# The out projection's last steps woven with norm, transposes and router in a written order, and low parts moved from GpSimd to VectorE

## The chip, the cores and the metric

The kernel runs on one core of a Trainium2 chip, as one program. The metric is the device time of one execution in microseconds. Besides the timed executions there is one profiled execution, and all rows below are from it. TensorE multiplies matrices, VectorE, ScalarE and GpSimd (POOL in the rows) work elementwise, and SyncE (SP) issues the loads of weights.

## What is computed

The reference is a chain of two blocks on 256 tokens of width 1024, all in float32. The first block has two layers of this form (the second block, attention with pooling and dense feed-forward parts, is untouched by the main part of the change):

```
mix = jnp.concatenate([ret_o, swa_o, mla_o], axis=-1) @ w_out[l]
x = layer_norm(DEEPNORM_ALPHA * x + mix, ln1_g[l], ln1_b[l])
ffn = grouped_moe(x, router_w, router_bias, exp_w_gate_up[l], exp_w_down[l])
x = layer_norm(DEEPNORM_ALPHA * x + ffn, ln2_g[l], ln2_b[l])
```

The three parts of `mix` are a retention, a sliding-window attention and a latent attention. The mixture of experts has 16 experts in 4 groups:

```
scores = jax.nn.sigmoid((t @ router_w).astype(jnp.float32))
biased = scores + router_bias.astype(jnp.float32)
grp = biased.reshape(T, N_GROUPS, EXPERTS_PER_GROUP)
grp_score = jnp.sum(lax.top_k(grp, TOP_K)[0], -1)
sel_group = jnp.argmax(grp_score, -1)
...
h = jnp.einsum('td,edf->tef', t, w_gate_up)
a = jax.nn.silu(h[..., :D_EXPERT]) * h[..., D_EXPERT:] * gates[..., None].astype(h.dtype)
y = jnp.einsum('tef,efd->td', a, w_down)
```

Each token picks one group, and two experts within it.

## The kernel before

Tokens are held in two halves t = 0, 1 of 128 each. All products are made to float32's accuracy from two parts of each operand, a high part (rounded) and a low part (the rest), in three passes: high by high, low by high, high by low. A weight tile is loaded (`raw`, 1 MB, line 336), its high part `whi` is made on ScalarE (L350) and its low part `wlo` on VectorE (L351), in pieces of 128x1024, of which five are held at a time. Two pieces come from one `raw`.

The stage in question lies between attention and experts, once in each layer. The out projection (`gemm_wide("wo", ...)`, results `oo`, one bank for each token half and half of the columns) runs over 8 contraction steps. Its last TAIL = 3 steps are grouped: all three for t = 0, then all three for t = 1, so that half 0 ends early. Then come, for each half, the residual on VectorE (L899), the statistics of the norm (`ln_stats`, L570 to L573, and a reciprocal square root of ten small ops, `ln1...`, L480 to L489), and 8 transposes of the token tile on TensorE (`trx`, L1053), copied to `rT` on ScalarE. `centre` normalizes the tokens on ScalarE (L1039), makes their high part there (L1040, `xs`) and the low part on GpSimd (L1041, `xs`).

`route` makes the logits from the transposes (`lg`, 16 matmuls in two passes each, 32 rows in the trace), keeps TensorE's clock up with 24 idle matmuls (`keep_clock(WARM[0])`, `idle`), takes the tanh on ScalarE, finds the groups on VectorE by small ops (L948 to L967; `rGb` is the choice of group), counts tokens of each group on TensorE (`cn`), and gives each token a slot. WARM[1] = 12 more idle matmuls follow. `pm` (L1064) is the permutation made of the slots. Then the tokens are gathered by group on TensorE (`og`, 8 tiles of four matmuls: low and high part, both halves), and `affine_evac` brings each tile to high part `xgh` (ScalarE, L605), a plain copy `aff` (VectorE, L606) and low part `xgl` (VectorE, L607). Products of expert 0 (`ogu<-whi,xgh` and so on, 24 matmuls for each expert's gate and up part) begin between the og.

After that the program has a branch (`tc.If(most > P)`) for the case that a group holds more than 128 tokens. The number is read by the engines from `mi`, which VectorE computes. Behind it stand the products that spread gates over slots (`gp`), the transposes `trp`, expert 1's products, the down products of expert 0 (`yg`), then expert 2 and so on.

The order of instructions on each engine is set by a scheduler that goes by priorities, except inside `tc.manual_schedule`, where the engines named take them in the order in which the code is written. `tc.issue_after` puts what it encloses behind a given instruction.

Of the kernel before, what the change touches and what calls it, by code (L numbers as in the profile page):

```python
# [19 lines left out]
P = 128  # L20
T = 256
D = 1024
KT = 8
# [343 lines left out]
def build(ctx: ExitStack, tc: tile.TileContext, ap, tap=None, parts=("b1", "b2")):  # L367
# [57 lines left out]
    def gemm_wide(name, x, nk, outs, order=None, nseg=1, tail=1):  # L425


        groups = [[i] for i in range(nk - tail)] + [list(range(nk - tail, nk))]
        for group in groups:
            ws = [[W.next(name) for s in range(nseg)] for i in group]  # L430
            for t in range(2):
                for i, w in zip(group, ws):
                    kt = order[i] if order else i
                    xa = tuple(h[:, kt, t * P : (t + 1) * P] for h in x[:2])
                    for s in range(nseg):
                        for o, c0, c1 in outs[t][s::nseg]:
                            mm3(o, xa, (w[s][0][:, c0:c1], w[s][1][:, c0:c1]), i == 0, i == nk - 1)
# [164 lines left out]
    def affine_evac(hi, lo, src, g, b, work):  # L602
# [53 lines left out]
    def attention1(l, x, hl, work, cb):  # L656
# [174 lines left out]
        for t in range(2):  # L831
# [4 lines left out]
            G.tensor_tensor(out=gg[:, t, :], in0=th, in1=rep("gn", l), op=ALU.mult)  # L836
# [42 lines left out]
        def score(h, sc):  # L879
# [11 lines left out]
        gemm_wide(  # L891
            "wo", mix, 8, [[(oo[t][n], n * 512, (n + 1) * 512) for n in range(2)] for t in range(2)], OUT_ORDER,
            tail=TAIL,
# [8 lines left out]
        return residual, router  # L902
# [19 lines left out]
    def route(rT, stats, router, work):  # L922


        gw, bs = router
        lg = bank("mm", "lg")
        lgs = work.tile([P, 2, NE], F32, name="lgs")
        for t in range(2):
            o = lg[:, t * NE : (t + 1) * NE]
            for kt in range(KT):  # L930
                last = mm(o, rT[:, t, kt, :], gw[:, kt, :], kt == 0, kt == KT - 1)
        with tc.issue_after(last.ins):
            keep_clock(WARM[0])
        for t in (1, 0):
            V.scalar_tensor_tensor(
                out=lgs[:, t], in0=lg[:, t * NE : (t + 1) * NE], scalar=stats[t][1], in1=bs, op0=ALU.mult, op1=ALU.add
# [8 lines left out]
        S.activation(out=sc.rearrange("p t g e -> p (t g e)"), in_=lgs.rearrange("p t e -> p (t e)"), func=AF.Tanh, scale=0.5)  # L945
        rb = rb5.rearrange("p (g e) -> p g e", g=4)
        for t in range(2):
            V.scalar_tensor_tensor(out=bi[:, t], in0=sc[:, t], scalar=0.5, in1=rb, op0=ALU.mult, op1=ALU.add)  # L948
# [18 lines left out]
        TT(out=G1, in0=key, in1=mx.unsqueeze(2).to_broadcast([P, 2, 4]), op=ALU.is_equal)  # L967
# [8 lines left out]
        last = mm(cn[:, 8:12], one, Gb[:, 1, :], False, True)  # L976
        with tc.issue_after(last.ins):
            keep_clock(WARM[1])
# [38 lines left out]
    def moe(l, residual, router):  # L1017

        with ExitStack() as es:
# [11 lines left out]

            def centre(t):

                mu, rs = stats[t]
                nb = tiny.tile([P, 1], F32, name="nb_ln1", tag="bnnb")
                V.scalar_tensor_tensor(out=nb, in0=mu, scalar=-1.0, in1=rs, op0=ALU.mult, op1=ALU.mult)
                for n in range(2):
                    c = slice(n * 512, (n + 1) * 512)
                    S.activation(out=r[:, t, c], in_=r[:, t, c], func=AF.Identity, scale=rs, bias=nb)  # L1039
                    S.copy(xs[t][:, 0, c], r[:, t, c])  # L1040
                    split = G.tensor_tensor(  # L1041
# [4 lines left out]
            for t in range(2):  # L1046
                r = residual(t)
                stats.append(ln_stats(r, t, "ln1"))
# [554 lines left out]
```

## Time and profile before

| what | value |
|---|---|
| three timed runs | 1735.08, 1733.93, 1735.04 us; median 1735.04 |
| profiled execution | 1737.42 us, its span 1735.6 us |
| TensorE busy | 1673.4 us, 96% of the span |
| VectorE, ScalarE, GpSimd busy | 1278.7, 988.0, 56.2 us |
| TensorE's wait `cn<-rGb` | 3.7 us in each of two layers |

A kernel whose TensorE is busy nearly all the time is read by the few stretches in which it is not, and by the clock it was granted in them: the windows view shows both.

### The profile page before, as it was taken

Reading aid. Unit: us, or ns where it says so; the run is one execution under the profiler, and the core shown is the slowest. Engines: PE = TensorE matmul, PEld = TensorE weight load, DVE = VectorE, ACT = ScalarE, POOL = GpSimd, SP = SyncE. Lnnn points to the kernel's source line nnn. Section 1 sums busy time; section 2 is a strip of 40 time slices with the busy share of each in tenths; the row PEclk is TensorE's granted clock in tenths of the full one; section 3 lists DMA queues with packets and bytes.
Section 4 is the critical chain, followed back from the end, with each engine's and each line's share of the span. In section 5 each row is a group of like instructions: output and inputs, shape, how many; then the busy total and the mean of one; then the engine's idle time right before and its main releaser. Section 6 shows DMA issues by size and latency. Waiting matters only on the chain.

```text
span 1735.6 us, 26627 instructions
## 1 busy us (share of the span) xinstructions
PE 1673.4 (96%) x10190; PEld 1458.9 (84%) x10190; DVE 1278.7 (74%) x2318; ACT 988.0 (57%) x1647; POOL 56.2 (3%) x52
## 2 busy tenths in 40 slices
PE   8998999899999989999999999999999999999997
PEld 8877777797777778999989989998999998988886
DVE  5768999876789987666865676667666775676666
ACT  5645777574577764455565544555555565465553
POOL 0001000200100000000000000000000000100000
PEclk9998999999899999999999999999999999999999
DMA  9432999553279864555533455554455452545540
GB/s 380 148 108 96 344 333 352 188 179 122 74 275 342 329 249 150 191 191 174 184 121 130 170 179 185 194 179 162 174 191 190 148 186 89 193 170 194 191 149 25
DMA packets 49141, 330.93 MB, mean 191 GB/s; under 512 B 5616, under 2 KB 5872, under 8 KB 13424
## 3 DMA queue, kind: packets, MB, share of 16 engines
q1 hardware_dynamic: 47664, 324.68, 51.6%
q10 hardware_dynamic: 1344, 4.49, 0.9%
q8 instruction: 82, 1.34, 0.3%
q14 instruction: 51, 0.42, 0.1%
HBM read 325.74 MB, written 1.05 MB: 188 GB/s over the span
## 4 chain that ended last, share of the span: by engine, by line
PE 67%; DVE 3%; ACT 1%; issue 1%; ACTq 0%; DVEq 0%
PE v L411 14%; PE f L411 14%; PE u L411 14%; PE ogt L411 6%; PE ogu L411 4%; PE oz L411 3%; PE obr L411 3%; PE yg L411 2%; PE ovp L411 2%; PE oq L411 2%; DVE wlo L351 1%; ACT whi L350 1%; PE sc L411 1%; PE po L411 1%; PE opl L411 1%
## 5 line engine op out<-in xcount | busy, mean ns | idle before, releaser
L351 DVE TENSOR_TENSOR wlo<-raw,whi 128x1024 fp32r<-128x1024 f32 (+2 forms) x611 | 736.4, 1212 | 319.0 <-ACT whi L350 303.5
L350 ACT CAST whi<-raw 128x1024 fp32r<-128x1024 f32 (+2 forms) x611 | 629.8, 1034 | 541.1 <-PE v L411 122.6
L411 PE MATMUL f<-fhh,whi 128*128 128x256 f32 x1056 | 196.5, 286 | 1.6 <-DVE fhh L1332 1.6
L411 PE MATMUL v<-xT_hf,whi 128*128 128x512 f32 x528 | 190.7, 399 | 5.4 <-DVE fhp L1329 5.4
L411 PE MATMUL u<-xT_hf,whi 128*128 128x512 f32 x528 | 189.3, 397 | 0.7 <-ACT htok L1314 0.7
L411 PEld LDWEIGHTS f<-fhh,whi 128*128 128x128 f32 x1056 | 166.4, 193 | 6.2 <-DVE fhh L1332 2.3
L411 PE MATMUL f<-fhh,wlo 128*128 128x256 f32 x528 | 149.9, 286 | 0.0
L411 PE MATMUL v<-xT_hf,wlo 128*128 128x256 f32 x528 | 148.5, 281 | 0.0
L411 PE MATMUL u<-xT_hf,wlo 128*128 128x256 f32 x528 | 148.3, 281 | 0.0
L411 PEld LDWEIGHTS v<-xT_hf,whi 128*128 128x128 f32 x528 | 99.7, 189 | 29.7 <-ACT fsl L1325 6.2
L411 PEld LDWEIGHTS u<-xT_hf,whi 128*128 128x128 f32 x528 | 99.1, 188 | 22.8 <-ACT htok L1314 0.9
L411 PE MATMUL ogu<-wlo,xgh 128*128 128x512 f32 x256 | 101.7, 397 | 4.3 <-DVE wlo L351 4.3
L411 PE MATMUL ogu<-whi,xgh 128*128 128x512 f32 x256 | 102.2, 399 | 0.1
L411 PEld LDWEIGHTS f<-fhh,wlo 128*128 128x128 f32 x528 | 101.3, 192 | 0.0
L411 PEld LDWEIGHTS u<-xT_hf,wlo 128*128 128x128 f32 x528 | 99.8, 189 | 1.0
L411 PEld LDWEIGHTS v<-xT_hf,wlo 128*128 128x128 f32 x528 | 100.3, 190 | 0.3
L411 PE MATMUL ogu<-whi,xgl 128*128 128x512 f32 x256 | 100.4, 392 | 0.0
L411 PE MATMUL ogt<-xT_hmx,whi 128*128 128x256 f32 x512 | 97.5, 287 | 0.0
L411 PE MATMUL yg<-whi,hh 128*128 128x512 f32 x256 | 84.6, 391 | 3.4 <-ACT hh L495 3.3
L411 PEld LDWEIGHTS ogt<-xT_hmx,whi 128*128 128x128 f32 x512 | 80.4, 191 | 3.0 <-issue 1.5
L411 PE MATMUL ogt<-xT_hmx,wlo 128*128 128x256 f32 x256 | 73.2, 287 | 0.0
L411 PE MATMUL v<-xT_h,whi 128*128 128x512 f32 x176 | 64.3, 403 | 2.7 <-DVE fhp L1329 2.7
(505 smaller groups left out, 3287.8 us busy)
## 6 DMA issues: line engine op xcount, KB each, us to landing
raw<-in_wflat_dram SPq DMA_DIRECT2D x276, 1024.0 KB, 4.8
raw<-in_wflat_dram SPq DMA_DIRECT2D x10, 960.0 KB, 4.7
raw<-in_wflat_dram SPq DMA_DIRECT2D x4, 992.0 KB, 4.8
gb<-in_rows_dram SPq DMA_DIRECT2D x6, 512.0 KB, 4.7
raw<-in_wflat_dram SPq DMA_DIRECT2D x4, 512.0 KB, 3.2
raw<-in_wflat_dram SPq DMA_DIRECT2D x2, 1008.0 KB, 6.1
raw<-in_wflat_dram SPq DMA_DIRECT2D x2, 976.0 KB, 6.8
raw<-in_wflat_dram SPq DMA_DIRECT2D x4, 384.0 KB, 6.1
```

What stands on the lines that cost most here:

```text
L350: nc.scalar.copy(hi[:, :n], r[:, c : c + n])
L351: self.split = nc.vector.tensor_tensor(out=lo[:, :n], in0=r[:, c : c + n], in1=hi[:, :n].bitcast(F32), op=ALU.subtract)
L411: return TE.matmul(out, lhsT=lhsT, rhs=rhs, start=start, stop=stop, skip_group_check=shared)
```

## The change

The code of the routing stage is written in a fixed order for TensorE and VectorE. `gemm_wide` hands out the last three out-projection steps as functions, so that the residual, transposes and logits of half 0 can stand between the steps of half 1. The reciprocal square root is made once for both halves, on 128x2. Both `centre` come behind the tanh. The low parts of the tokens move from GpSimd to VectorE, behind `pm` (`rest`). In `affine_evac` of this stage every second tile's `aff` moves from VectorE to ScalarE. Outside the stage, three multiplies and sums move from GpSimd to VectorE: the cosine multiply of rope, the retention's `gg`, and the mixer's `msum`.

```diff
+        def step(t, i, w):
+            kt = order[i] if order else i
+            xa = tuple(h[:, kt, t * P : (t + 1) * P] for h in x[:2])
...
+            if defer and group is groups[-1]:
+                return [[lambda t=t, i=i, w=w: step(t, i, w) for i, w in zip(group, ws)] for t in range(2)]
...
         S.activation(out=hi, in_=src, func=AF.Identity, scale=g, bias=b)
-        V.tensor_scalar(out=tmp, in0=src, scalar1=g, scalar2=b, op0=ALU.mult, op1=ALU.add)
+        if turn:
+            S.activation(out=tmp, in_=src, func=AF.Identity, scale=g, bias=b)
+        else:
+            V.tensor_scalar(out=tmp, in0=src, scalar1=g, scalar2=b, op0=ALU.mult, op1=ALU.add)
...
-        G.tensor_tensor(out=dst, in0=src, in1=cosT.unsqueeze(1).to_broadcast(shape), op=ALU.mult)
+        V.tensor_tensor(out=dst, in0=src, in1=cosT.unsqueeze(1).to_broadcast(shape), op=ALU.mult)
...
-            G.tensor_tensor(out=gg[:, t, :], in0=th, in1=rep("gn", l), op=ALU.mult)
+            V.tensor_tensor(out=gg[:, t, :], in0=th, in1=rep("gn", l), op=ALU.mult)
...
-                    split = G.tensor_tensor(
+            def rest(t):
+
+                for n in range(2):
+                    c = slice(n * 512, (n + 1) * 512)
+                    split = V.tensor_tensor(
                         out=xs[t][:, 1, c], in0=r[:, t, c], in1=xs[t][:, 0, c].bitcast(F32), op=ALU.subtract
                     )
...
+            with tc.manual_schedule(engines={mybir.EngineType.PE, V.engine}):
+                for f in steps[0]:
+                    f()
+                r = residual(0)
+                moments(0)
+                steps[1][0]()
+                turned(0)
+                steps[1][1]()
+                logits(rT, 0, lg, router[0])
+                steps[1][2]()
+                r = residual(1)
+                turned(1)
+                moments(1)
+                V.tensor_scalar(out=ve, in0=mv[:, :, 1], scalar1=LN_EPS, scalar2=None, op0=ALU.add)
+                rsqrt_n(ve, rs, 2, 1.0)
+                logits(rT, 1, lg, router[0])
+                keep_clock(WARM[0])
...
+                with tc.high_priority(offset=200):
+                    G1, slot, tot, late = route(lg, rs, router, work)
+                with tc.issue_after(routed.ins):
+                    centre(0)
+                    centre(1)
...
+                rest(0)
+                split = rest(1)
...
-            G.tensor_tensor(out=ms, in0=mg[:, :T], in1=mg[:, T:], op=ALU.add)
+            V.tensor_tensor(out=ms, in0=mg[:, :T], in1=mg[:, T:], op=ALU.add)
```

What this moves on the engines is seen best in their queues. First VectorE between the last attention output (`mixT`) and the second half's statistics, before:

```order
L351 TENSOR_TENSOR wlo<-raw,whi 128x1024
L496 TENSOR_TENSOR mixT<-po,mixT 128x256
L899 SCALAR_TENSOR_TENSOR x_133<-x_133,oo_1318 128x512
L899 SCALAR_TENSOR_TENSOR x_133<-x_133,oo_1319 128x512
L570 BN_STATS st_ln_1470<-x_133 128x6 x2
L571 BN_AGGR mv_ln_1471<-st_ln_1470 128x2
L573 TENSOR_SCALAR ve_ln_1475<-mv_ln_1471 128x1
L480 TENSOR_SCALAR ln10i<-ve_ln_1475 128x1
L351 TENSOR_TENSOR wlo<-raw,whi 128x1024
L481 TENSOR_SCALAR ln10y<-ln10i 128x1
L899 SCALAR_TENSOR_TENSOR x_133<-x_133,oo_1320 128x512
```

and the same place of the changed kernel:

```order
L503 TENSOR_TENSOR mixT<-po,mixT 128x256
L909 SCALAR_TENSOR_TENSOR x_133<-x_133,oo_1318 128x512
L909 SCALAR_TENSOR_TENSOR x_133<-x_133,oo_1319 128x512
L1047 BN_STATS st_ln_1460<-x_133 128x6 x2
L1048 BN_AGGR mv_1432<-st_ln_1460 128x2
L909 SCALAR_TENSOR_TENSOR x_133<-x_133,oo_1320 128x512
L909 SCALAR_TENSOR_TENSOR x_133<-x_133,oo_1321 128x512
L1047 BN_STATS st_ln_1516<-x_133 128x6 x2
```

The two `wlo` shown, and three more around them, are gone from here. VectorE behind the slots, in the changed kernel (L1063 makes the low parts `xs`, L616 is `aff`, L617 `xgl`):

```order
L1107 TENSOR_SCALAR pm<-cperm,rslot 128x512 x2
L1063 TENSOR_TENSOR xs_1430<-x_133,xs_1430 128x512 x2
L1004 TENSOR_TENSOR rpk<-rsc,rG 128x16
L1063 TENSOR_TENSOR xs_1431<-x_133,xs_1431 128x512 x2
L351 TENSOR_TENSOR wlo<-raw,whi 128x1024
L616 TENSOR_SCALAR aff<-og,cols 128x512
L351 TENSOR_TENSOR wlo<-raw,whi 128x1024
L617 TENSOR_TENSOR xgl<-aff,xgh 128x512 x2
L616 TENSOR_SCALAR aff<-og,cols 128x512
L351 TENSOR_TENSOR wlo<-raw,whi 128x1024
L617 TENSOR_TENSOR xgl<-aff,xgh 128x512 x2
```

The pattern goes on to a fourth `wlo` and the eighth `xgl`; behind that stand gate ops with six more `wlo` among them, the third of which is expert 1's first, and then the branch. Before, `pm` was followed by the gate ops, then `aff` and `xgl` with no `wlo` between them, and one `wlo` ahead of the branch. TensorE where the out projection ends, in the changed kernel:

```order
L1073 MATMUL trx<-cperm,x_133 128x128 x8
L411 MATMUL oo_1320<-whi,mixT 128x512
L411 MATMUL oo_1320<-wlo,mixT 128x512
L411 MATMUL oo_1320<-whi,mixT 128x512
L411 MATMUL oo_1321<-whi,mixT 128x512
L411 MATMUL oo_1321<-wlo,mixT 128x512
L411 MATMUL oo_1321<-whi,mixT 128x512
L411 MATMUL lg<-gw,rT 128x16 x8
```

Before, all 16 `trx` and then all 16 `lg` stood behind the last `oo`. Ahead of the branch, TensorE now has 17 of the 24 matmuls of expert 1: one between those of expert 0, and 16 in a row behind them, of which the last four are here:

```order
L411 MATMUL ogu<-wlo,xgh 128x512
L411 MATMUL ogu<-whi,xgl 128x512
L411 MATMUL ogu<-whi,xgh 128x512
L411 MATMUL ogu<-wlo,xgh 128x512
L1161 TENSOR_LOAD mi
L1163 COMPARE_AND_BRANCH
```

Before, none of them stood there: behind expert 0's products came the zeroing of `ya` and then the branch.

## Rows read from the trace of the kernel before

**Rows 1.** The page: busy time, share of the span and instructions of each engine.

```profile
PE 1673.4 (96%) x10190; PEld 1458.9 (84%) x10190; DVE 1278.7 (74%) x2318; ACT 988.0 (57%) x1647; POOL 56.2 (3%) x52
```

**Rows 2.** Timeline of TensorE, layer 0: start, length, operation, idle before and releaser.

```profile
134.37 0.39 PE L411 MATMUL oo<-wlo,mixT 128*128 128x512 f32 x1
134.60 0.39 PE L411 MATMUL oo<-whi,mixT 128*128 128x512 f32 x1
...
136.61 4.04 PE L411 MATMUL lg<-gw,rT 128*128 128x16 f32 x32
140.49 4.15 PE L411 MATMUL idle<-zeros 128*128 128x256 bf16 x24
...
148.53 0.27 PE L411 MATMUL cn<-rGb,cntw 128*128 128x4 bf16 x5 [3.67 <-DVE rGb L966]
148.67 2.72 PE L411 MATMUL idle<-zeros 128*128 128x256 bf16 x12
151.04 4.20 PE L411 MATMUL og<-pm,xs 128*128 128x512 f32 x12
...
166.76 1.92 PE L411 MATMUL gp<-rvs,pm 128*128 128x4 f32 x16 [0.64 <-PEq L1118]
...
174.18 0.50 PE L411 MATMUL yg<-whi,hh 128*128 128x512 f32 x1 [0.71 <-ACT hh L495]
...
179.53 0.39 PE L411 MATMUL ogu<-whi,xgh 128*128 128x512 f32 x1
```

**Rows 3.** Windows: busy time of each engine, granted clock, DMA share, GB/s.

```profile
148.50:151.00 2.50, 2.47 (x17) 1.78 (x17) 2.47 (x22) 0.00 (x0) 0.00 (x0) 0.50 0.00 0
151.00:155.20 4.20, 4.20 (x15) 3.40 (x14) 2.46 (x16) 1.56 (x2) 0.00 (x0) 0.69 0.02 6
...
179.50:200.00 20.50, 20.50 (x93) 16.39 (x92) 19.25 (x20) 16.25 (x20) 0.00 (x0) 1.00 1.00 368
...
465.00:467.50 2.50, 2.48 (x17) 1.79 (x17) 2.47 (x22) 0.00 (x0) 0.00 (x0) 0.50 0.00 0
```

**Rows 4.** Timeline of TensorE, layer 1: cn, and the first matmul of expert 2.

```profile
465.02 0.28 PE L411 MATMUL cn<-rGb,cntw 128*128 128x4 bf16 x5 [3.66 <-DVE rGb L966]
...
497.13 0.39 PE L411 MATMUL ogu<-whi,xgh 128*128 128x512 f32 x1
```

**Rows 5.** Timeline of VectorE, layer 0, from the residual to the permutation.

```profile
135.32 0.68 DVE L899 SCALAR_TENSOR_TENSOR x<-x,oo 128x512 f32<-128x512 f32 x1
...
142.87 0.84 DVE L948 SCALAR_TENSOR_TENSOR rbi<-rsc,rb 128x16 f32<-128x16 f32 x2 [0.52 <-ACT rsc L945]
143.74 1.14 DVE L952 TENSOR_TENSOR rpr<-rbi 128x16 f32<-128x16 f32 x1
...
148.31 0.17 DVE L966 TENSOR_TENSOR rGb<-cperm,rmx 128x8 bf16<-128x8 f32 x1
...
149.29 0.88 DVE L1064 TENSOR_SCALAR pm<-cperm,rslot 128x512 fp32r<-128x512 f32 x2
```

**Rows 6.** Timeline of GpSimd, layer 0: low parts of the tokens.

```profile
142.32 5.02 POOL L1041 TENSOR_TENSOR xs<-x,xs 128x512 fp32r<-128x512 f32 x4 [1.12 <-ACT xs L1040]
```

**Rows 7.** Timeline of VectorE in another stage: one op of the two-column root.

```profile
659.10 0.16 DVE L467 TENSOR_TENSOR rva<-rvb 128x2 f32<-128x2 f32 x1
```

**Rows 8.** Timeline of ScalarE, layer 0: four copies of the transposes.

```profile
135.98 2.04 ACT L1055 COPY rT<-trx 128x512 f32<-128x512 f32 x4
```

**Rows 9.** Timeline of VectorE, layer 0, gathered tokens and weights' low parts.

```profile
155.40 1.52 DVE L606 TENSOR_SCALAR aff<-og,cols 128x512 f32<-128x512 f32 x2
156.84 1.28 DVE L607 TENSOR_TENSOR xgl<-aff,xgh 128x512 fp32r<-128x512 f32 x2
...
168.81 2.35 DVE L351 TENSOR_TENSOR wlo<-raw,whi 128x1024 fp32r<-128x1024 f32 x2
```

**Rows 10.** Groups of GpSimd's instructions: busy us, mean ns of one, idle before.

```profile
L1472 POOL TENSOR_TENSOR msum<-mg 128x256 f32<-128x256 f32 x16 | 12.8, 800 | 207.1 <-DVE mg L1470 207.1
```

**Rows 11.** Waits of TensorE, layer 1's attention stage: us in total, times, longest.

```profile
PE oret L411 <- DVE sT L847: 1.1, 2, 0.6
```

More of the change, by code (lines that the diff above doesn't have):

```diff
@@ L900, in residual @@
             return x
-        return residual, router
+        return residual, router, steps
     def router_weights(l, work):
@@ L920, in router_weights, with logits, route @@
         return gw, sums[:, 1]
-    def route(rT, stats, router, work):
-        gw, bs = router
-        lg = bank("mm", "lg")
-        lgs = work.tile([P, 2, NE], F32, name="lgs")
[L928 to L933, printed above, removed]
+    def logits(rT, t, lg, gw):
+        for kt in range(KT):
+            mm(lg[:, t * NE : (t + 1) * NE], rT[:, t, kt, :], gw[:, kt, :], kt == 0, kt == KT - 1)
+    routed = None
+    def route(lg, rs, router, work):
+        bs = router[1]
+        lgs = work.tile([P, 2, NE], F32, name="lgs")
         for t in (1, 0):
             V.scalar_tensor_tensor(
-                out=lgs[:, t], in0=lg[:, t * NE : (t + 1) * NE], scalar=stats[t][1], in1=bs, op0=ALU.mult, op1=ALU.add
+                out=lgs[:, t], in0=lg[:, t * NE : (t + 1) * NE], scalar=rs[:, t : t + 1], in1=bs, op0=ALU.mult, op1=ALU.add
             )
@@ L975, in route @@
         mm(cn[:, 8:12], one, Gb[:, 0, :], False, False)
-        last = mm(cn[:, 8:12], one, Gb[:, 1, :], False, True)
-        with tc.issue_after(last.ins):
-            keep_clock(WARM[1])
+        mm(cn[:, 8:12], one, Gb[:, 1, :], False, True)
+        keep_clock(WARM[1])
+        TT(out=G1, in0=key, in1=mx.unsqueeze(2).to_broadcast([P, 2, 4]), op=ALU.is_equal)
         tot = w([4], "rtot")
@@ L1015, in route, with moe @@
         return G1, slot, tot, gates
-    def moe(l, residual, router):
+    def moe(l, residual, router, steps):
         with ExitStack() as es:
@@ L1044, in centre, with turned @@
                 return split
-            for t in range(2):
-                r = residual(t)
-                stats.append(ln_stats(r, t, "ln1"))
+            def turned(t):
                 for k4 in range(2):
-                    tr = bank("acc", "trx")
+                    tr = bank("tr", "trx")
                     for j in range(4):
@@ L1053, in moe @@
                         TE.transpose(tr[:, j * P : (j + 1) * P], r[:, t, kt * P : (kt + 1) * P], ident)
-                    with tc.high_priority(offset=200):
-                        S.copy(rT[:, t, 4 * k4 : 4 * k4 + 4, :].rearrange("p k s -> p (k s)"), tr)
-                if t == 0:
-                    centre(0)
-            G1, slot, tot, late = route(rT, stats, router, work)
-            split = centre(1)
-            tap(f"G{l}", G1)
-            pm = work.tile([P, 2, 4, P], F32R, name="pm")
@@ L1063, in moe @@
-            for t in range(2):
-                routed = V.tensor_scalar(
-                    out=pm[:, t].rearrange("p g s -> p (g s)"), in0=iota, scalar1=slot[:, t : t + 1],
-                    scalar2=None, op0=ALU.is_equal,
-                )
+                    S.copy(rT[:, t, 4 * k4 : 4 * k4 + 4, :].rearrange("p k s -> p (k s)"), tr)
+            lg = bank("mm", "lg")
+            rs = work.tile([P, 2], F32, name="rs1")
+            nb = work.tile([P, 2], F32, name="nb1")
+            ve = work.tile([P, 2], F32, name="ve1")
@@ L1078, in moe @@
                     affine_evac(
-                        xgh[:, kt, :], xgl[:, kt, :], o, col("ln1_g", l, kt), col("ln1_b", l, kt), work
+                        xgh[:, kt, :], xgl[:, kt, :], o, col("ln1_g", l, kt), col("ln1_b", l, kt), work, kt % 2
                     )
@@ L1513, in build @@
             cb = work.tile([P, ap["cb1"].shape[1]], F32, name="cb1")
-            residual, router = attention1(l, x, hl, work, cb)
-        r2 = moe(l, residual, router)
+            residual, router, steps = attention1(l, x, hl, work, cb)
+        r2 = moe(l, residual, router, steps)
         xh = ln_hat(r2, "ln2")
```

47 lines of the change are left out of this document (30 added, 17 removed).

## The prediction

> **What bounds the kernel now.** I read the page first: TensorE is busy 96% of the span [rows 1], so a change can pay only in the few places where TensorE stands still or runs slowly. The list of its waits then names the routing stage, once in each of the two layers, and the timeline of TensorE through that stage, layer 0 first, is what the rest is read from. The reader is to see there the end of the out projection (oo), 16 transposes, the router logits (lg), 24 idle matmuls, then 3.67 us in which the counting matmul cn waits for rGb from VectorE, 12 idle matmuls, the gather og, the first products after the branch (gp), and at 179.53 the first matmul of expert 2 [rows 2]. I call that last moment M. Behind it TensorE is busy 20.50 of 20.50 us [rows 3], so a shift of M shifts the end one to one. In layer 1 the cn wait is as long, 316.49 us later, and M is 497.13 [rows 4], or 180.64 by layer 0's time.
>
> The clock is the second thing to see. After the 3.67 us wait the granted share is 0.50 (the 1.2 GHz level) from 148.5 to 151 and 0.69 from 151 to 155.2, and layer 1 shows 0.50 again [rows 3]; twelve idle matmuls take 2.72 us where 24 took 4.15, and the first 12 og take 4.20 us, where passes at the full clock are 0.23 us apart (134.37 to 134.60), or 2.8 us [rows 2]. So the half clock costs 0.65 + 1.4 = 2.1 us a layer.
>
> The third is VectorE before rGb: two small ops take 0.84 and the next 1.14 us, and two more of that size as long, [rows 5] exactly while GpSimd makes the low parts xs, from 142.32 to 147.34 [rows 6]; outside that stretch an op of that size takes 0.17 us (rGb itself). Some 3 us of the cn wait come from that.
>
> **The change, part by part.** *Up to the slots.* TensorE now does 8 transposes and 8 logits steps of token half 0 between the out projection's last steps of half 1. That is half of what lies between the last oo's end, 134.99, and the first idle matmul, 140.49 [rows 2], or 2.8 us, and the oo of half 1 ends so much later: 137.8. VectorE then has the residual (two ops of 0.68 [rows 5], the first partly before that), two statistics of like length, and aggregate: to 140.2. One rsqrt for both halves, ten dependent ops on 128x2, at about 0.2 us each (0.16 busy [rows 7] and a step between): to 142.2. The logits and tanh take to rbi 0.8 to 1.0 us, to 143.1; then the chain to rGb without GpSimd beside it, about ten ops at 0.2: 145.1, against 148.31. TensorE meanwhile: transposes of half 1 to 139.3, two copies rT on ScalarE of 0.51 each [rows 8], eight logits steps of 2.0 us, to 141.9, and 24 idle matmuls, 4.15: 146.05. So cn no longer waits for VectorE; it is the idle matmuls that end last. From cn to the first pm 0.76 us as before, and both pm 0.88 [rows 5]: they end at 147.7 instead of 150.2. **Gain so far 2.5 us, and the half clock of before is gone as well.**
>
> *Behind the slots.* The gain is spent here. VectorE now makes the low parts xs: four ops like xgl, 1.28 for two [rows 9], 2.6 us in all, to 150.3. The five wlo that stood among and ahead of the residual and norm ops (where VectorE's queue had room, since it waited there for oo) now stand behind xs. In the queue from there to the low part of expert 1's first weight piece I count 7 wlo at 1.18 (2.35 for two), 4 aff at 0.76, 8 xgl at 0.64 [rows 9], and some 15 small gate ops at 0.11 (between rGb and the first pm nine steps take 0.98 us [rows 5]): 8.2 + 3.0 + 5.1 + 1.6 = 17.9, to 168.2. Four aff at 0.76 went to ScalarE, otherwise it would be 171.2; ScalarE, busy 57% of the span [rows 1], has time for them. TensorE can run only as far as the eighth xgl, which lies 3 wlo and 13 small ops before that, at 163.2, and two passes on. It then waits with `ogu<-wlo` of expert 1 from about 163.6 to 168.2, **4.6 us (3.5 to 5.2) of new wait in place of the 3.67 us removed**. Queued behind that matmul are 15 more of expert 1, and then the branch, which reads mi; mi itself stands behind two further wlo on VectorE, so it is ready at about 171.0.
>
> From there to M at full clock: 16 passes paced by the two further wlo, to 171.8; 0.64 for the branch, as ahead of gp before; gp at 172.4. From gp to M it was 12.8 us (166.76 to 179.53), of which 17 of expert 1's 24 passes at 0.23 now stand ahead of the branch, 3.9, and the wait for hh, 0.71 [rows 2], is covered by the passes that stand around it: 8.2. **M = 180.6.** If the VectorE ops start as closely as in their densest rows (wlo at 1.14, small ops at 0.09) and pm ends with them, 179.0; if every third of them waits a little for its operand, 181.7. Against 179.53 and 180.64 that is +1.1 and −0.05: together +1.0, bounds −2.2 to +3.2.
>
> *The clock after the new wait.* No row of before has this wait, but the nearest, 3.67 us, was followed by the half clock in both layers. So I take it that TensorE again comes out of 4.6 us at 1.2 GHz. What that cost before was 2.1 us; here the first 16 passes are partly paced by wlo anyway, so I take 1.7 a layer, bounds 0 and 2.5: **+3.4**. The Trainium skill says in "TensorE: Matmul & The Clock Gate", section "What's actually happening", that the throttled clock is the default and that activity releases it; that speaks against this change, since it puts TensorE's idle time in front of dense work and not in front of idle matmuls. The trace agrees, with 0.50 behind the 3.67 us. By the rule the sum is the one below; if the clock stayed up, it would be 3.4 less.
>
> *The rest.* gg moves from GpSimd to VectorE, and its two ops stand between th and the decay product sT, for which TensorE already waits 1.1 us in two times in layer 1 [rows 11]: about 0.3 us more a layer, 0 to 0.6: +0.6. Rope's cosine multiply (four ops) and the mixer's 16 msum (0.80 each on GpSimd [rows 10]) become VectorE work, by xgl's 0.64 for 512 columns an estimated 0.3 for an msum and 1.3 to 1.6 for a rope op. What hides them is that TensorE never waits for either's result; with that cover gone they would cost at most 16 × 0.3 + 4 × 1.5 = 10.8 us. I take 0. The merged rbi, the later G1 and nb are in the chain above.
>
> Sum: +1.0 + 3.4 + 0.6 = +5.0. The profiled execution took 1737.42 us (span 1735.6, and 1.8 around it that the change leaves alone), so it becomes 1742.4; the three timed runs have their median 2.4 below it, 1735.04, so the forecast is **1740.0**.
>
> **The rivals.** *A: the clock stays at 2.4 GHz after the new wait.* Then +1.6, 1736.6, no measurable change (0.2%, 3.5 us, is about what a measurement of this kernel can tell). For it: TensorE has been working, if with gaps, for 10 us before. Against it: both waits of 3.7 us were followed by 0.50. The rule named above would not let this happen.
>
> *B: faster.* The gain of 2.5 us in pm is kept, because the weights' low parts don't end last. The place is the wait for expert 1's wlo; it decides as soon as that wait is under about 2 us, since then there is no half clock either, M falls by 2.5 us in the mean of the layers, and the time is 1735.0 − 5 + 0.6 = 1730.6. If VectorE cost nothing there, TensorE's own work (some 26.3 us from og to M: 28.5 before, from 151.04 to 179.53, less 1.4 of half clock and some 0.8 of waits) would give M = 174.2, 6 us a layer, and about 1724. For it: GpSimd no longer slows VectorE, and four aff at 0.76 left its queue. Against it: 18 us of queued VectorE work, each term from a row, stand between 150.3 and that piece, in an order that can't change at run time.
>
> *C: the moves off GpSimd end last.* sT late by the whole of gg and msum late in part, +2 to +5 on top: 1742 to 1745. Against: TensorE's waits there are short or none.
>
> *D: nothing at all,* both ends cancelling at M: this lies within A's range.
>
> **How the numbers follow.** Forecast 0.47, A and D 0.30, B 0.17, C 0.06. The forecast's own range is 1737 to 1743: a few of its cases lie within 0.2% (0.04), C is slower. So slower 0.49, same 0.33, faster 0.18 (with a little of A's lower end). The range reaches from B's middle to above the forecast's upper bound: 1731 to 1743.5.
>
> **What would show it.** Right: no cn wait for rGb (idle matmuls run into cn); the small ops after tanh at 0.2 us; no GpSimd row there; pm ending near 147.7; then in TensorE's waits `ogu <- wlo`, about 4 to 5 us, once a layer just before the branch, and the granted share 0.5 to 0.7 in the 4 us behind it; M near 182.3 and, in layer 1, 182.3 + 316.5. Wrong: that wait under 2 us, or the share at 1.00 behind it, or pm no earlier than 149 (then copies or tanh are later than summed). If M is as said and the end is not, it is the retention stage or the mixer, and the waits for sT or msum must show it.

## The result and the profile after

The changed kernel takes 1747.8 us (median of 4 runs, 1746.3 to 1750.97), the kernel before beside it 1734.68 (4 runs, 1733.93 to 1735.08). The ratio is 1.0074 (95% interval 1.0058 to 1.0090): slower, and by more than the 1740.0 of the forecast and its range. In a second measurement (e10) the ratio was 1.0086 (1.0069 to 1.0103). The profiled execution of the changed kernel took 1746.3 us with a span of 1744.5, against 1737.42 and 1735.6 before. So the spans differ by 8.9 us and the medians by 13.1. The 4.2 between them come from the profiled runs' places: before's lies 2.7 above the median of its runs here, after's 1.5 below. No trace accounts for that part.

The page first, the same row as [rows 1]: busy time, share of the span and instructions of each engine. GpSimd has shrunk from 56.2 to 18.0 us, and TensorE's busy time has grown by 3.4 us with the same 10190 instructions, which says that some of them ran at a lower clock.

```profile
PE 1676.8 (96%) x10190; PEld 1459.1 (84%) x10190; DVE 1275.8 (73%) x2324; ACT 989.5 (57%) x1653; POOL 18.0 (1%) x20
```

TensorE's timeline through the routing stage of layer 0, to be laid beside [rows 2]:

```profile
137.62 0.40 PE L411 MATMUL oo<-whi,mixT 128*128 128x512 f32 x1
138.11 1.35 PE L1073 MATMUL trx<-cperm,x 128*128 128x128 f32 x8
...
141.52 4.37 PE L411 MATMUL idle<-zeros 128*128 128x256 bf16 x24
...
145.75 0.26 PE L411 MATMUL cn<-rGb,cntw 128*128 128x4 bf16 x5
145.94 1.47 PE L411 MATMUL idle<-zeros 128*128 128x256 bf16 x12
147.17 3.83 PE L411 MATMUL og<-pm,xs 128*128 128x512 f32 x15
...
166.81 0.79 PE L411 MATMUL ogu<-wlo,xgh 128*128 128x512 f32 x1 [3.88 <-DVE wlo L351]
...
173.48 2.00 PE L411 MATMUL gp<-rvs,pm 128*128 128x4 f32 x16 [0.30 <-PEq L1163]
...
182.70 0.39 PE L411 MATMUL ogu<-whi,xgh 128*128 128x512 f32 x1
```

The wait of cn is gone, and og starts at 147.17 where it started at 151.04. Some 15 us later TensorE stands for 3.88 us for a low part wlo, and M has moved from 179.53 to 182.70. Layer 1 repeats it, where M was 497.13 [rows 4]:

```profile
489.61 0.79 PE L411 MATMUL ogu<-wlo,xgh 128*128 128x512 f32 x1 [3.89 <-DVE wlo L351]
...
497.38 1.92 PE L411 MATMUL gp<-rvs,pm 128*128 128x4 f32 x16 [2.30 <-issue]
...
506.28 0.39 PE L411 MATMUL ogu<-whi,xgh 128*128 128x512 f32 x1
```

VectorE in layer 0 says why the piece is late. The chain reaches rGb at 144.95 instead of 148.31 [rows 5], pm has both its ops done by 147.38, and the low parts xs follow. Then the queue runs almost without a gap to the wlo that TensorE waits for, which ends at 166.75:

```profile
144.95 0.17 DVE L977 TENSOR_TENSOR rGb<-cperm,rmx 128x8 bf16<-128x8 f32 x1
...
146.50 0.88 DVE L1107 TENSOR_SCALAR pm<-cperm,rslot 128x512 fp32r<-128x512 f32 x2
147.29 1.29 DVE L1063 TENSOR_TENSOR xs<-x,xs 128x512 fp32r<-128x512 f32 x2
...
149.79 1.22 DVE L351 TENSOR_TENSOR wlo<-raw,whi 128x1024 fp32r<-128x1024 f32 x1
...
165.53 1.22 DVE L351 TENSOR_TENSOR wlo<-raw,whi 128x1024 fp32r<-128x1024 f32 x1
```

The windows show the clock, to be laid beside [rows 3] (window, TensorE, weight load, VectorE, ScalarE and GpSimd busy, granted clock, DMA share, GB/s). Before the wait it is 1.00. Behind it, it is 0.50, the 1.2 GHz level, and it is 0.50 again behind the branch, where TensorE had stood still for only 0.30 us (the gp row of layer 0 above). The last row belongs to the other stage that grew, the retention stage of layer 1:

```profile
147.20:151.00 3.80, 3.80 (x18) 2.92 (x17) 3.80 (x8) 2.04 (x4) 0.00 (x0) 1.00 0.00 0
...
169.00:172.00 3.00, 3.00 (x8) 2.31 (x8) 1.96 (x6) 1.14 (x2) 0.00 (x0) 0.50 0.99 404
175.90:178.90 3.00, 3.00 (x12) 2.51 (x11) 1.32 (x2) 1.54 (x3) 0.00 (x0) 0.50 0.84 309
...
415.00:423.00 8.00, 8.00 (x27) 6.41 (x27) 1.53 (x6) 0.00 (x0) 0.00 (x0) 0.50 0.28 116
```

In the kernel before, the same matmuls lie some 3.5 us earlier, and their window reads 0.79:

```profile
411.50:419.50 8.00, 8.00 (x34) 6.66 (x34) 4.41 (x18) 0.38 (x1) 0.00 (x0) 0.79 0.21 85
```

TensorE's timeline there, first after, then before. Each oret is six products with a decay tile sT that VectorE makes:

```profile
409.18 0.92 PE L411 MATMUL scr<-rq 64*128 64x256 f32 x4
...
412.01 0.88 PE L411 MATMUL oret<-vv,sT 128*128 128x64 f32 x6 [1.15 <-DVE sT L857]
...
414.38 1.52 PE L411 MATMUL oret<-vv,sT 128*128 128x64 f32 x6 [0.64 <-DVE sT L857]
...
433.75 0.33 PE L885 MATMUL trr<-cperm,ro 128*128 128x128 f32 x1 [0.72 <-DVE ro L881]
```

```profile
405.66 0.92 PE L411 MATMUL scr<-rq 64*128 64x256 f32 x4
...
407.82 0.88 PE L411 MATMUL oret<-vv,sT 128*128 128x64 f32 x6 [0.48 <-DVE sT L847]
...
410.20 0.88 PE L411 MATMUL oret<-vv,sT 128*128 128x64 f32 x6 [0.64 <-DVE sT L847]
...
426.46 0.33 PE L875 MATMUL trr<-cperm,ro 128*128 128x128 f32 x1 [0.72 <-DVE ro L871]
```

And VectorE after, just before that first oret: the two gg ops now stand ahead of sT.

```profile
410.73 0.75 DVE L846 TENSOR_TENSOR gg<-th,reps 128x256 f32<-128x256 f32 x2
411.40 0.55 DVE L857 TENSOR_TENSOR sT<-scr,cb 128x384 f32<-128x384 f32 x1
```

The wait for sT has grown by 0.67 us (0.48 to 1.15); in layer 0 the two waits have grown together by 0.88, from 0.22 to 1.10. The second oret takes 1.52 instead of 0.88, with the same six products, and from the first scr to the first trr the stage takes 24.57 us instead of 20.80.

**Where the 8.9 us went.** The markers are the first scr, the first trr, and M in each layer; each row is the length after minus the length before.

| Stretch | Before | After | Difference |
|---|---|---|---|
| start to first scr, layer 0 | 91.69 | 91.08 | −0.61 |
| retention, layer 0 | 18.28 | 19.19 | +0.91 |
| first trr to M, layer 0 | 69.56 | 72.43 | +2.87 |
| M to first scr of layer 1 | 226.13 | 226.48 | +0.35 |
| retention, layer 1 | 20.80 | 24.57 | +3.77 |
| first trr to M, layer 1 | 70.67 | 72.53 | +1.86 |
| M to the end | 1238.47 | 1238.22 | −0.25 |

So the routing stage cost 4.7 us, the retention stage as much again, and all else −0.5.

### The profile page after: what moved, and what is told of

The parts are those of the page before. It is cut to its first block, busy times and chain, and to the rows that moved or that the text cites. A ratio compares the mean times of both kernels' runs of the same rounds, so it can differ in the third digit from the quotient of the medians.

```text
span 1744.5 us, 26540 instructions
## 1 busy us (share of the span) xinstructions
PE 1676.8 (96%) x10190; PEld 1459.1 (84%) x10190; DVE 1275.8 (73%) x2324; ACT 989.5 (57%) x1653; POOL 18.0 (1%) x20
## 3 DMA queue, kind: packets, MB, share of 16 engines
HBM read 325.74 MB, written 1.05 MB: 187 GB/s over the span
## 4 chain that ended last, share of the span: by engine, by line
PE 67%; DVE 3%; ACT 1%; issue 0%; ACTq 0%; DVEq 0%
PE v L411 14%; PE f L411 14%; PE u L411 14%; PE ogt L411 6%; PE ogu L411 4%; PE oz L411 3%; PE obr L411 3%; PE yg L411 2%; PE ovp L411 2%; PE oq L411 2%; DVE wlo L351 1%; PE sc L411 1%; PE po L411 1%; ACT whi L350 1%; PE opl L411 1%
## 5 line engine op out<-in xcount | busy, mean ns | idle before, releaser
L411 PEld LDWEIGHTS f<-fhh,whi 128*128 128x128 f32 x1056 | 166.8, 193 | 6.1 <-DVE fhh L1377 2.3
L411 PEld LDWEIGHTS ogu<-wlo,xgh 128*128 128x128 f32 x256 | 49.6, 194 | 24.8 <-DVE wlo L351 14.1
```

What stands on the lines that cost most here:

```text
L411: return TE.matmul(out, lhsT=lhsT, rhs=rhs, start=start, stop=stop, skip_group_check=shared)
```

## The experiments

The theory: two losses that have nothing to do with each other. In the routing stage the low parts of expert 1's weights come too late, because a hint binds their start to the token splits. In the retention stage gg delays sT a little, and the clock falls. Rivals: the VectorE time of xs or of aff itself is the loss; the clock behind the wait is all of it; rope or msum on VectorE cost something. The ratios below are against the kernel before on the same chip; the prices in us compare the medians, except where a stretch of a trace is named.

**e1: without the hint.** The fetch of each weight piece stands inside a hint that lets its instructions be issued only after `split`, the last op that makes a low part of the tokens. That line is in the kernel before too, but there `split` is a GpSimd instruction.

```diff
-                    with tc.issue_after(split.ins):
-                        w = W.next("gu")
+                    w = W.next("gu")
```

> The changed kernel without the hint that puts the first expert weights behind the last low part of the tokens (that instruction is on GpSimd before and on VectorE in the change, so the hint now holds VectorE's queue). Five low parts of weights go back among the residual and norm ops; all else stays. If VectorE's queue of low parts is what takes the gain away: no wait of TensorE for expert 1's low part, no half clock behind it, first matmul of expert 2 near 176 in layer 0 instead of 182.7, and near 500 instead of 506.3 in layer 1; time about 1734 (1731 to 1737), 12 to 15 below the changed kernel. If the low parts of the tokens on VectorE or the written order itself cost the time: first matmul of expert 2 within 2 us of 182.7 and the time above 1743.

Measured: 1738.66 us, 12 runs, ratio 1.0011 (0.9998 to 1.0023). The long wait for wlo is gone in both layers (the longest is 0.5 us), and from the first trr to M it takes 66.8 and 67.6 us, 2.8 and 3.1 less than before and 5.7 and 4.9 less than after. The wlo return among the residual and norm ops, with no regard to rGb (VectorE's timeline, then TensorE's in both layers):

```profile
138.72 1.22 DVE L351 TENSOR_TENSOR wlo<-raw,whi 128x1024 fp32r<-128x1024 f32 x1
139.85 0.68 DVE L909 SCALAR_TENSOR_TENSOR x<-x,oo 128x512 f32<-128x512 f32 x1
...
141.65 1.21 DVE L351 TENSOR_TENSOR wlo<-raw,whi 128x1024 fp32r<-128x1024 f32 x1
```

```profile
148.06 0.27 PE L411 MATMUL cn<-rGb,cntw 128*128 128x4 bf16 x5 [0.55 <-DVE rGb L977]
...
468.04 0.27 PE L411 MATMUL cn<-rGb,cntw 128*128 128x4 bf16 x5 [2.03 <-DVE rGb L977]
```

So the hint is the cause of the new wait. M comes at 177.81 and 498.83, near what was expected, but the time is above the expected range and no better than before's. The trace says where the rest is: retention takes 19.2 and 25.8 us here, 0.9 and 5.0 more than before, which eats up the routing stage's gain. The span is 3.6 us longer than before's, nearly all of it in two other stretches, 1.5 between M and layer 1's retention and 1.9 behind the second M; no run shows what lengthens these.

**e2: low parts back on GpSimd.** Everything else as in the change.

```diff
-                    split = V.tensor_tensor(
+                    split = G.tensor_tensor(
```

> The changed kernel with only the low parts of the tokens back on GpSimd; the same hint then names a GpSimd instruction. If it is the hint's move of the weights' low parts that costs: the five stand early again, no wait for expert 1's low part, first matmul of expert 2 near 177 to 179 in layer 0 (GpSimd takes 5 us for the low parts, now from about 146 on, and the gather's low passes wait for them), time about 1738 (1735 to 1741). If it is the interleaved out projection that costs, no change against the changed kernel: 1746 to 1749.

Measured: 1739.58 us, 12 runs, ratio 1.0021 (1.0007 to 1.0034). The hint now names a GpSimd instruction again and the wlo go early, as in e1. What GpSimd costs its neighbour shows on VectorE (GpSimd's row first, a timeline each):

```profile
147.20 5.38 POOL L1063 TENSOR_TENSOR xs<-x,xs 128x512 fp32r<-128x512 f32 x4 [3.74 <-DVE rG L988]
```

```profile
147.24 1.36 DVE L1004 TENSOR_TENSOR rpk<-rbi,rG 128x16 f32<-128x16 f32 x2
...
148.95 2.49 DVE L1107 TENSOR_SCALAR pm<-cperm,rslot 128x512 fp32r<-128x512 f32 x2
```

The two pm take 2.49 us beside xs and 0.88 without. The Trainium skill says in "GPSIMD Engine Reference", section "1. Specifications", that GpSimd shares its SBUF interfaces with VectorE and contends with VectorE instructions that have two inputs in SBUF or run in a two-port mode. The trace agrees for rpk with its two inputs (1.36 for two, 0.26 in the changed kernel); which mode pm runs in, no run here shows. From trr to M it is 69.8 in both layers, 0.3 more and 0.9 less than before. Against e1, where the wlo go early too but xs is on VectorE, that is 3.1 and 2.1 us more, less than the hint's 5.7 and 4.9 (after against e1). These are lengths from one trace each, and the next experiment shows them to vary by some 2 us with the stage's code unchanged. The medians of e1 and e2 differ by 0.9 us only, so what GpSimd costs in time is not shown; the hint costs about 10 us by the medians (e1's 1738.66 against 1748.66 of e10).

**e3: gg back on GpSimd.** Everything else as in the change.

```diff
-            V.tensor_tensor(out=gg[:, t, :], in0=th, in1=rep("gn", l), op=ALU.mult)
+            G.tensor_tensor(out=gg[:, t, :], in0=th, in1=rep("gn", l), op=ALU.mult)
```

> The changed kernel with the retention's gate multiply back on GpSimd. If its two VectorE ops, 0.7 us ahead of the decay product, are what lengthened layer 1's retention by 3.8 us (through the wait and a longer stretch of half clock): waits of TensorE for the decay product back to 0.5 and 0.6 in layer 1 and 0.2 in layer 0, the stretch at 0.50 back to some 4 us, time about 1744 (4 less than the changed kernel). If the half clock there comes and goes by chance: waits shorter by 1.2 in all but the half clock as long, time 1746 to 1748.

Measured: 1742.41 us, 12 runs, ratio 1.0037 (1.0026 to 1.0048). Retention is back at 18.3 and 20.8 us, exactly before's lengths, and so is the wait:

```profile
409.89 0.88 PE L411 MATMUL oret<-vv,sT 128*128 128x64 f32 x6 [0.48 <-DVE sT L857]
```

Between 1.0037 here and 1.0074 or 1.0086 for the whole change lie 0.4 to 0.5%, 6 to 9 us, for two ops in each layer. The routing stage, whose code the edit leaves alone, takes 70.7 and 75.0 us here where it took 72.4 and 72.5 after: in layer 0 no half clock follows the branch, in layer 1 TensorE waits 1.62 us there and the half clock lasts longer. A difference of some 2 us in one layer's stage, read from one trace, is thus no proof of an effect.

**e6: gg alone, in the kernel before.** The same edit the other way round, and nothing else of the change.

```diff
-            G.tensor_tensor(out=gg[:, t, :], in0=th, in1=rep("gn", l), op=ALU.mult)
+            V.tensor_tensor(out=gg[:, t, :], in0=th, in1=rep("gn", l), op=ALU.mult)
```

> The kernel before with only the retention's gate multiply on VectorE. If it alone lengthens the retention: waits for the decay product 0.5 and 0.6 in layer 0 and 1.15 and 0.6 in layer 1, retention 0.9 longer in layer 0 and 3 to 5 longer in layer 1 (half clock of some 10 us), time about 1740. If the half clock is by chance: 1736 to 1737, by the waits alone (1.2 us).

Measured: 1741.58 us, 5 runs, ratio 1.0031 (1.0018 to 1.0043), 5.8 us above before's 1735.8. Retention takes 23.9 and 25.8 us, with the half clock in both layers. The windows of e6 in layer 0 and 1; in the kernel before, the first of them reads 1.00:

```profile
97.00:103.00 6.00, 6.00 (x21) 5.08 (x21) 1.92 (x7) 0.00 (x0) 0.00 (x0) 0.50 0.03 10
414.00:422.00 8.00, 7.65 (x26) 6.16 (x26) 1.72 (x4) 0.00 (x0) 0.00 (x0) 0.50 0.29 120
```

So gg's move makes the kernel slower by itself, with no help from the rest. The growth in layer 0, 5.6 us where 0.9 was expected, comes with a half clock that the changed kernel did not have there. The two retention stages of this trace add 10.6 us and the span is only 6.4 longer, so the price is the medians' 5.8 and not the sum of the stages.

**e4: idle matmuls in the gap.** The wait stays, but 22 idle matmuls stand behind expert 0's last product, so that TensorE waits less at a stretch. The scheduler did one thing more: all 24 of expert 1's matmuls now stand ahead of the branch, 23 of them in a row behind the wait, where the changed kernel has 17 and 16.

```diff
-                    mm3(o0, (xgh[:, i, :P], xgl[:, i, :P]), w, i == 0, i == KT - 1)
+                    done = mm3(o0, (xgh[:, i, :P], xgl[:, i, :P]), w, i == 0, i == KT - 1)
+            with tc.issue_after(done.ins), tc.high_priority(offset=200):
+                keep_clock(22)
```

> The changed kernel with 22 idle matmuls (3.8 us at the full clock) behind expert 0's last product, so that TensorE works in the new wait without anything useful. VectorE's queue is as in the changed kernel. If the half clock costs as I forecast, and more since it returns behind the branch: granted share near 1.00 from 163 on, expert 1's passes 0.23 apart, first matmul of expert 2 near 180.3 and 503.5, time about 1743 (4 to 5 less). If the wait alone sets the time (passes paced by the low parts at either clock): share 1.00, but expert 2 within 0.7 us of the changed kernel and the time unchanged.

Measured: 1743.43 us, 6 runs, ratio 1.0046 (1.0029 to 1.0063). TensorE's timeline, then the windows:

```profile
164.93 2.58 PE L411 MATMUL idle<-zeros 128*128 128x256 bf16 x22
...
168.97 0.50 PE L411 MATMUL ogu<-wlo,xgh 128*128 128x512 f32 x1 [1.46 <-DVE wlo L351]
...
177.77 3.54 PE L411 MATMUL gp<-rvs,pm 128*128 128x4 f32 x16 [3.29 <-PEq L1165]
```

```profile
169.00:174.00 5.00, 5.00 (x22) 4.15 (x23) 4.96 (x11) 2.95 (x3) 0.00 (x0) 1.00 0.94 377
178.00:182.00 4.00, 4.00 (x20) 4.00 (x21) 0.61 (x3) 0.00 (x0) 0.00 (x0) 0.50 0.93 352
```

With the gap filled the clock stays at 1.00 behind it, in both layers: the half clock there comes from TensorE standing still. M is at 187.09 and 504.40, which fits neither of the two cases in layer 0. In layer 1 the way from trr to M is 1.5 us shorter than after (71.05 against 72.53). In layer 0 TensorE then waits 3.29 us behind the branch, and the half clock comes there instead; that way is 2.2 us longer. Both differences are within what e3 shows without any edit to the stage, so a gain from the idle matmuls is not shown. The median is some 4 us below after's 1747.8, but this run's retention in layer 1 (19.9 us, 4.7 less than after's, at a granted 1.00, with the wait for sT as long as after) has a share in that which the idle matmuls can't explain.

**e5: without the hint, and gg back.** Both causes undone, e1 and e3 together.

> The changed kernel without the hint and with the retention's gate multiply back on GpSimd: both suspected costs undone, the written order, the low parts on VectorE, the aff turn, rope and msum kept. If those two are the whole of the loss and add up: retention as long as before (18.3 and 20.8 us from the first scr to the first trr), route stage from the first trr to expert 2 near 66.8 and 67.6 (before 69.6 and 70.7), time about 1730 (1728 to 1732), faster than before by 0.2 to 0.4%. If the clock takes the gain back elsewhere, or the two overlap: 1734 to 1737.

Measured: 1735.36 us, 12 runs, ratio 0.9990 (0.9981 to 1.0000). That is 5 us above the first case and inside the second. The wait for wlo and gg's delay of sT are gone, but the time is before's:

```profile
147.08 0.27 PE L411 MATMUL cn<-rGb,cntw 128*128 128x4 bf16 x5 [2.21 <-DVE rGb L977]
```

The wlo that return among the norm ops make rGb late by 2.21 and 2.0 us, and in layer 0 the half clock is back behind cn (0.50 from 147.0 to 149.6). The routing stage is still 1.5 and 3.3 us shorter than before (68.1 and 67.3). The trace loses this in three other places: 1.6 us in layer 1's retention, which takes 22.4 with the same waits for sT as before and a lower clock, 1.6 between M and that retention, and 2.2 behind the second M. What lengthens the last two is not shown; two profiles of the changed kernel (after and e10) differ by 3.0 behind the second M. As long as the place of the wlo is left to the scheduler, the interleaving brought no measurable time.

**e7: all affine ops on VectorE.** In the change, half of the eight aff go to ScalarE. This puts them back, to see whether the wait is the length of VectorE's queue.

```diff
-    xgh[:, kt, :], xgl[:, kt, :], o, col("ln1_g", l, kt), col("ln1_b", l, kt), work, kt % 2
+    xgh[:, kt, :], xgl[:, kt, :], o, col("ln1_g", l, kt), col("ln1_b", l, kt), work, 0
```

> The changed kernel with all eight aff on VectorE again, so that its queue ahead of expert 1's low part is four ops of 0.76, some 3 us, longer. If that queue ends last: the wait for expert 1's low part grows from 3.9 to about 4 to 7 us or expert 0's passes are later by as much, and expert 2 starts 2.5 to 3.5 us later in each layer, one time about 1752. If ScalarE's queue was the bound (aff on it is gone now): expert 2 no later than in the changed kernel.

Measured: one run, 1752.14 us, span 1750.3. The wait splits, into about 0.76, 1.32 and 3.82 us in each layer, and from trr to M it is 2.4 and 4.8 us longer than after, for four more aff of 0.72 us (2.9 us). The wait follows the queue; the size is from one run.

**e8: rope and msum alone, in the kernel before.** The rest of what left GpSimd.

```diff
-        G.tensor_tensor(out=dst, in0=src, in1=cosT.unsqueeze(1).to_broadcast(shape), op=ALU.mult)
+        V.tensor_tensor(out=dst, in0=src, in1=cosT.unsqueeze(1).to_broadcast(shape), op=ALU.mult)
...
-            G.tensor_tensor(out=ms, in0=mg[:, :T], in1=mg[:, T:], op=ALU.add)
+            V.tensor_tensor(out=ms, in0=mg[:, :T], in1=mg[:, T:], op=ALU.add)
```

> The kernel before with only rope's cosine multiply and the mixer's sum on VectorE. As forecast, hidden: time within 0.1% of before (1734 to 1737). If they end last somewhere: up to 10 us more, with a wait of TensorE in the mixer or in the stage of the latent attention that was not there before.

Measured: 1736.03 us, 10 runs, ratio 1.0000 (0.9991 to 1.0009). An msum takes 424 ns on VectorE where it took 800 on GpSimd [rows 10], a rope multiply 1.21 to 1.49 us instead of 2.85 to 2.97, and TensorE waits for neither.

**e9: a version that puts the wlo where VectorE has room.** The interleaving is kept and gg stays on GpSimd. The weights of expert 0's eight contraction steps, four low parts wlo, are fetched in the written order: two wlo ahead of the residual of token half 0 and two behind its statistics. The first down pieces wait for the low parts of the tokens.

```diff
-            V.tensor_tensor(out=gg[:, t, :], in0=th, in1=rep("gn", l), op=ALU.mult)
+            G.tensor_tensor(out=gg[:, t, :], in0=th, in1=rep("gn", l), op=ALU.mult)
...
+                ahead = [W.next("gu") for _ in range(4)]
                 r = residual(0)
                 moments(0)
+                ahead += [W.next("gu") for _ in range(4)]
...
-                        w = W.next("gu")
+                        w = ahead.pop(0) if ahead else W.next("gu")
...
-            pend = finish(0, o0, [W.next("dn") for _ in range(2)])
+            with tc.issue_after(split.ins):
+                first = [W.next("dn") for _ in range(2)]
+            pend = finish(0, o0, first)
```

> The changed kernel with expert 0's four low parts of weights written into the order (two ahead of half 0's residual, two between the halves' residuals, where VectorE waits for TensorE anyway), the down pieces held behind the low parts of the tokens, and the retention's gate multiply back on GpSimd. Against the kernel without the hint, no low part stands behind half 1's residual, so cn should wait at most 1 us (2.0 to 2.2 there) and the clock stay up through the gather. If the rest of the loss is that wait: route stage from the first trr to expert 2 near 65 to 66.5 us in both layers (69.6 and 70.7 before), time about 1731 (1728 to 1734). If the second half of the loss is chance of the clock elsewhere: 1734 to 1737.

Measured: 1727.68 us, 6 runs, ratio 0.9954 (0.9938 to 0.9970): faster than both kernels, 7.5 us below before's 1735.19, and just under the expected range. The first two low parts (at 121.81 and 126.37) lie where the kernel before had two. The third and the fourth now fall into time in which VectorE waits for oo, between the residuals of the two halves, and no wlo stands between half 1's residual and pm. VectorE's timeline of e9, then one of the two wlo that the kernel before had behind half 1's residual:

```profile
129.52 1.37 DVE L909 SCALAR_TENSOR_TENSOR x<-x,oo 128x512 f32<-128x512 f32 x2 [1.59 <-PE oo L411]
...
132.65 1.23 DVE L351 TENSOR_TENSOR wlo<-raw,whi 128x1024 fp32r<-128x1024 f32 x1 [0.32 <-ACT whi L350]
134.89 1.22 DVE L351 TENSOR_TENSOR wlo<-raw,whi 128x1024 fp32r<-128x1024 f32 x1 [1.02 <-ACT whi L350]
136.29 1.37 DVE L909 SCALAR_TENSOR_TENSOR x<-x,oo 128x512 f32<-128x512 f32 x2 [0.17 <-PE oo L411]
```

```profile
137.38 1.21 DVE L351 TENSOR_TENSOR wlo<-raw,whi 128x1024 fp32r<-128x1024 f32 x1
```

TensorE's timeline: cn waits 1.05 us, and M is 5.5 us ahead of before's in layer 0 and 7.2 in layer 1. The routing stage itself takes 64.8 and 66.1 us, 4.7 and 4.6 less than before; retention takes 18.3 and 22.4.

```profile
144.20 0.26 PE L411 MATMUL cn<-rGb,cntw 128*128 128x4 bf16 x5 [1.05 <-DVE rGb L977]
...
161.07 2.23 PE L411 MATMUL gp<-rvs,pm 128*128 128x4 f32 x16 [1.22 <-ACTq L1165]
...
174.06 0.40 PE L411 MATMUL ogu<-whi,xgh 128*128 128x512 f32 x1
...
489.93 0.40 PE L411 MATMUL ogu<-whi,xgh 128*128 128x512 f32 x1
```

Behind cn the granted clock is 1.00 in both layers; layer 0's window:

```profile
144.00:152.00 8.00, 7.80 (x44) 6.23 (x44) 7.92 (x32) 6.81 (x12) 0.00 (x0) 1.00 0.01 2
```

A half clock remains behind the branch, 0.50 from 162.6 to 165.9, which the kernel before did not have (1.00 from 166.8 to 179.5). So the stage is not yet as short as it can be.

**e10: the changed kernel again, beside e9.**

> The changed kernel once more, beside the others on the same chip, to see how its times scatter. By both theories 1746 to 1751, and the waits for expert 1's low part 3.9 us in both layers; if the half clock of layer 1's retention comes and goes, a second group of times some 3 to 4 us lower.

Measured: 1748.66 us, 4 runs (1743.51 to 1752.69), ratio 1.0086 (1.0069 to 1.0103). The wait for wlo is 3.88 us again and retention 19.2 and 24.5. The profiled run is the fastest of the four, and its retention of layer 1 has the half clock all the same, so a shorter stage there is not what made it the fastest.

## Why the prediction was wrong, step by step

**Up to the slots: right.** Forecast: oo ends at 137.8, rGb at 145.1, cn follows the idle matmuls at 146.05, pm ends at 147.7. Measured: 138.02, 145.12, 145.75, 147.38. Layer 1 had 0.85 us of wait for rGb left, since its 24 idle matmuls ended sooner: 2.78 us there, 4.37 in layer 0, where part of them ran at 0.50.

**The order of the queue behind the slots: right, with its cause not named.** Between xs and the end of the wlo in question the trace has the 7 wlo, 4 aff and 8 xgl that were counted, and it took 17.0 us for them and the small ops (149.79 to 166.75, with gaps) where 17.9 were reckoned. The new wait is 3.88 and 3.89 us against 4.6 (3.5 to 5.2). What the text did not say is why the wlo stand there: the unchanged hint on `split`. As a GpSimd instruction it didn't order VectorE's queue; as a VectorE instruction it does. e1 shows that.

**The clock behind the wait: right, and in part elsewhere.** Forecast 0.5 to 0.7; measured 0.50, from 166.8 to 172 in layer 0 and from 489.6 to 492.6 in layer 1. Passes there are 0.427 us apart instead of 0.23, which for the 11 steps from 167.40 to 172.09 makes 2.2 us and for the 6 from 490.21 to 492.77 1.2. e4 shows that standing still is what brings it. A second stretch at 0.50, behind the branch, was not foreseen: from gp to M it took 9.2 and 8.9 us where 8.2 were reckoned. Standing still does not explain that one, since TensorE had stood for only 0.30 us ahead of it in layer 0 and e9 has it too; what brings it, no run shows. With the 2.2 us in place of 1.7 it makes up for the 1.4 us by which the wait ended earlier than said. The rule of the Trainium skill in "TensorE: Matmul & The Clock Gate", section "What's actually happening", that the throttled clock is the default and activity releases it, agrees with the windows behind the wlo wait.

**M: right, but for an offset in layer 1.** Forecast 182.3 in layer 0; measured 182.70. For layer 1 the text said 316.5 us later, 498.8, and it is 506.28: that line left out that layer 0's own shift (3.17 at M) lies ahead of layer 1, and the retention stage adds 3.77. The routing stage taken alone cost 2.87 + 1.86 = 4.7 us against the forecast's 1.0 + 3.4 = 4.4.

**Rope, msum and the mixer: right.** Behind M of layer 1 the kernel is 0.25 us shorter than before, and e8 measures 1.0000.

**The term that failed: "The rest", +0.6 for gg.** The text said that sT would be about 0.3 us later in each layer, 0 to 0.6. That gg makes sT late was right, but the waits grew by 0.88 us in layer 0 and 0.67 in layer 1, both above the bound. And the term counted only the wait and left out what the same text had charged for the other wait, the clock behind it. In layer 0 the wait is all of the growth of 0.9, at a clock of 1.00; in layer 1 retention grew by 3.8, and 3.1 of that is the half clock. Together that is 4.7 instead of 0.6; e6 prices the move alone at 5.8 us, and e3 shows both the wait and the lengths back at before's. Why the clock falls there in most of the runs and not in all is open (last section). Rival C named this move with +2 to +5 and gave it 0.06, with the argument that the waits there are short. They are; but two of them follow each other within 3 us in layer 1 (1.15 and 0.64, ahead of 412.01 and 414.38), TensorE is busy for 2.85 of the 4 us from 409 to 413, and the 8 us behind ran at 0.50. With +4.7 in place of +0.6 the sum on the span is +9.1, and it measured +8.9.

**The median.** The forecast took the median 2.4 us below the profiled run's time. The changed kernel's median lies 1.5 above its own profiled run, so 3.9 of the 7.8 us by which 1747.8 misses 1740.0 come from there, and 3.9 from the span (8.9 against 5.0). The changed kernel's times are spread further (1743.5 to 1752.7 in its second measurement) than before's (1731.9 to 1737.7 beside it). That the clock in the retention stage varies from run to run may be a part of it; there is one trace for each measurement, so it stays open.

**What was not followed up, and could have been:** that rival B's gain was there to be had, by an order of the wlo and not by faster ops. Rival B reckoned that M would fall by 2.5 us where the wait is under 2 us, and by 6 us if VectorE cost nothing there. In e9 the routing stage is 4.7 and 4.6 us shorter than before: no half clock follows cn, and TensorE stands still for no more than 1.22 us at a time in the stage.

## What to carry to other kernels

A hint that orders work behind an instruction means something else when that instruction changes its engine: it then holds that engine's own queue, so look at every hint on an instruction that is moved. Price a wait with the clock behind it, also where it grows by less than 1 us: here 0.67 us more of wait went with 3.8 us more of the stage. And when work goes to a queue that has room in one place, write the order so that the work stands in that place; undoing the causes alone gave 0.9990, placing the low parts 0.9954.

## What the runs showed of the hardware that was not expected

- The clock in the retention stage isn't decided by the wait alone. In layer 1, with gg on VectorE (after, e1, e2, e4, e6, e7, e10) the stage took 24.6, 25.8, 24.2, 19.9, 25.8, 24.5 and 24.5 us, with gg on GpSimd (before, e3, e5, e8, e9) 20.8, 20.8, 22.4, 20.8 and 22.4. The first wait for sT in layer 1 was 1.15 us in e1, e2, e4, e6 and e7 alike, but in e4 no half clock followed (granted 1.00 from 419.5 to 427.5, the same place in the stage). In layer 0 it was 19.2 in five of the seven, and 20.7 and 23.9 in e4 and e6.
- TensorE's idle time ahead of gp, just behind the branch, differs between 0.30 and 3.29 us with no wait for data that would explain it: 0.64 before, 0.30 and 2.30 after in the two layers, 3.29 and 1.19 in e4, 1.22 in e9. After the longest of them the clock was 0.50 for 4 us; but it fell to 0.50 behind 0.30 us after, and stayed at 1.00 behind 0.64 us before, so the length of this wait alone does not decide it.
- GpSimd's 128x512 subtraction slows a pair of VectorE's 128x512 ops from 0.88 to 2.49 us.
